# A hybrid mixer kernel on one Trainium2 core: the background modulation taken 1024 columns at a time, in two loads

## The chip, the core and the metric

The kernel runs on one core of a Trainium2 chip. The metric is the device time of one execution in microseconds (us). Five engines work side by side, each through its own queue in a fixed order: TensorE (PE; its weight loads are shown as PEld), VectorE (DVE), ScalarE (ACT), GpSimd (POOL) and SyncE (SP), which issues the DMAs here.

## The reference

Two layers of a diffusion block over 256 context and 1024 latent tokens of width 1024. Before a layer's input is projected, it is normalized and modulated by a vector per stream (one for the latent tokens, one for the context), which comes out of one matrix product per layer:

```python
mod = jax.nn.silu(c) @ w_mod[l] + b_mod[l]            # w_mod[l] is (1024, 3072)
mod_c = jax.nn.silu(c_ctx) @ w_mod[l] + b_mod[l]
sh, sc, gt = jnp.split(mod, 3, axis=-1)               # three parts of 1024 columns
...
hx = _rms(x, norm_w[l]) * (1.0 + sc[:, None, :]) + sh[:, None, :]
ux = _split(hx @ w_in[l], [M_COLS, A_COLS, G_COLS, D_COLS])
outs = [_mlstm_mixer(...), _diff_mixer(...), _gla_mixer(...), _gdn_mixer(...)]
yx = jnp.concatenate([o[1] for o in outs], axis=-1)
x = x + gt[:, None, :] * (yx @ w_out[l])
```

The four mixers are an mLSTM, a differential attention, a gated linear attention (GLA) and a gated DeltaNet. Each takes its own columns of the projection.

## The kernel before

The program is written as strands: functions that each issue their instructions in their own order. A planner (`Issue`) runs while the program is built. It keeps a clock for each engine and for the DMA link, gives every instruction a due time by a rule of costs, and lets the strand go next whose instruction can start first; at equal times the lower rank goes. What comes out is one fixed order for each engine. A change in one strand therefore moves the instructions of all others around it.

In layer 0 two main strands run beside each other. `left` projects the input: products with `w_in` into PSUM tiles `mm`, the lowest-priority work, which fills PE between everything else. When its last product is issued and stored, `left` goes on with the mLSTM: first its states, ten tiles one after another (`m<-k_ident,kq` are a tile's transposes, `m<-pd` its state products), then its outputs (the first is `pp<-kq`). `right` runs a chain: the gates, the DeltaNet with its front (convolutions), decays (`e`), block products (`p<-K`, `po<-K`), an inverse on DVE and POOL (`Y`, `Z`, `ltmp`) and a scan (`p<-S,wq` to `po<-vn,at`); then the attention (`sc<-KT,qt` are its scores), then the GLA (`pd<-qm,km` its first products, `pd<-gv,inner` and `pd<-us,gq` its output products). The output projection is the last: its first half (`o<-w,yT`) beside the mLSTM, the rest after it. Layer 1 goes the same way.

The modulation is a strand of its own. Parts 0 and 1 of layer 0 are needed at once; `modulation` computes them in the first 53 us, 1024 columns wide, one load of 512 KB per step k and four matmuls, which write partitions 0, 32, 64 and 96 of the PSUM tile `ps` (`tile_position=(0, 32 * j)`). The other four parts (part 2 of layer 0, parts 0 to 2 of layer 1) run in the background, at rank 0, from a pool with three buffers `wm` of 128 x 512. Each part is two calls of 512 columns, one after the other; a call takes eight steps, each with one load of 256 KB and two matmuls of 256 columns, and ends with the copies out of `ps` and, for a gate (part 2), with the load of `b_mod`, an addition and the store to `gtd`. A load stands on SP's queue where the strand issues it, after the matmuls of the step before. When all are through, the strand sets "modulated". Two others wait for that: the DeltaNet's inverse before its products on PE, and `QK.rest`, which normalizes and rotates the keys and queries for the attention (two tiles of tokens at a time: load `x`, square, `ss`, the products with `rtk` or `rtq`, transposes `mm<-k_ident,x`, `hi` and `lo`) and uses the room that the modulation's pool gives back.

Of the kernel before, what the change touches and what calls it, by code (L numbers as in the profile page):

```python
# [22 lines left out]
DM = 1024  # L23
# [396 lines left out]
def _build(tc, nc, A, out, root, dbg):  # L420
    q_ = Issue()
    q_.log = dbg.get("log")
    V, S, G, P = (Eng(q_, e, r) for e, r in zip("VSGP", (nc.vector, nc.scalar, nc.gpsimd, nc.tensor)))
# [32 lines left out]
    def mark(label):  # L456
        if q_.me:
            q_.me.label = label

    def dma(dst, src):  # L460
        SP.dma_start(out=dst, in_=src)
# [58 lines left out]
    cvec = cst([128, 8, 2], "cvec")  # L520
# [6 lines left out]
    with ExitStack() as st:  # L527
        ps = Pool(st, "crps", PSUM)([128, 512], "tr")[:, :16]
# [38 lines left out]
    def pc(l, key, i=0, n=1):  # L567
        return pcol[:, l, PR[key] + i:PR[key] + i + n]
# [31 lines left out]
        return A["x"][0, 128 * (t - NCT):128 * (t - NCT) + 128, :]  # L600


    def modulation(l, part, c0, n, p, pps, bufs):

        ps = pps([128, 256], "mod")
        for k in range(8):
            w = p([128, n], "wm", bufs)
            dma(w, A["w_mod"][l, 128 * k:128 * k + 128, 1024 * part + c0:1024 * part + c0 + n])
            if (l, part, k) == (0, 1, 7):
                q_.set("w_mod loads")  # L610
            for j in range(n // 256):
                P.matmul(ps[32 * j:32 * j + 2], cvec[:, k, :], w[:, 256 * j:256 * j + 256],
                         start=(k == 0), stop=(k == 7), tile_position=(0, 32 * j))
        q_.need(("params", l))
        rows = p([128, n], "wm", bufs)[:2].rearrange("p (a b) -> p a b", b=256)
        for j in range(n // 256):
            V.tensor_copy(rows[:, j, :], ps[32 * j:32 * j + 2])
        if part < 2:
            m, k0 = n // 128, c0 // 128
            pt = pps([128, 256], "mod")  # L620
            for j in range(m):
                P.transpose(pt[:, 2 * j:2 * j + 2], rows[:, j // 2, 128 * (j % 2):128 * (j % 2) + 128], ident[:2, :2])
            md = p([128, 8, 2], "md")[:, :m]
            V.tensor_tensor(md, pt[:, :2 * m].rearrange("p (k v) -> p k v", v=2),
                            pc(l, "bm", 8 * part + k0, m).unsqueeze(2).to_broadcast([128, m, 2]), ALU.add)
            for v in range(2):
                if part == 1:
                    V.scalar_tensor_tensor(AB[l][:, 0, v, k0:k0 + m], md[:, :, v], 1.0, pc(l, "nw", k0, m), ALU.add, ALU.mult)
                else:
                    V.tensor_copy(AB[l][:, 1, v, k0:k0 + m], md[:, :, v])  # L630
        else:
            brow = p([128, n], "wm", bufs)[:2]
            dma(brow, A["b_mod"][l:l + 1, 2048 + c0:2048 + c0 + n].to_broadcast([2, n]))
            rv = rows.rearrange("p a b -> p (a b)")
            V.tensor_tensor(rv, rv, brow, ALU.add)
            dma(gtd[l][:, c0:c0 + n], rv)

    def first_norm(hT):
# [6 lines left out]
        def modulations():  # L645
            mark("0mod")
            with ExitStack() as st:
                mp, mps = Pool(st, "wm", side="right"), Pool(st, "mps", PSUM, "right")
                for part in range(2):
                    modulation(0, part, 0, DM, mp, mps, 5)  # L650
            q_.set((0, "AB"))
            q_.need((0, "normed"))

            q_.me.rank = RANK["mod"]
            with ExitStack() as st:
                mp, mps = Pool(st, "wm"), Pool(st, "mps", PSUM)
                q_.set((0, "room"))
                for l, part in ((0, 2), *((l, part) for l in layers if l for part in range(3))):
                    for c0 in (0, 512):
                        modulation(l, part, c0, 512, mp, mps, 3)  # L660
                if "d" in parts:
                    q_.need((0, "front"))
            q_.set("modulated")
        q_.spawn(0, modulations)
        if True:
            st2 = ExitStack()
            xp, pps = Pool(st2, "xn"), Pool(st2, "nps", PSUM)
# [39 lines left out]
        for i in range(len(todo) + 2):  # L707
            if i < len(todo):
                g, k = todo[i]
# [3 lines left out]
            if 0 < i <= len(todo):  # L713
                g, k = todo[i - 1]
                S.copy(hT[0][g][:, k, :], flat[g][:, k, :])
            if i > 1:
                g, k = todo[i - 2]
# [2198 lines left out]
```

## Time and profile before

| | |
|---|---|
| time, median of 3 runs | 2483.91 us (2483.13 to 2484.88) |
| the profiled execution, its own time | 2481.02 us |
| its span, first to last instruction | 2479.1 us |
| PE busy | 2194.1 us, 89% of the span |
| background modulation on PE | from 91.1 us to 339.5 us |
| last gate row of it stored | 342.62 us |
| attention of layer 0, first scores | 686.79 us |
| layer 0's projections end on PE | about 1057 us |
| first mLSTM output product of layer 0 | 1156.01 us |

The trace is one execution. Times of it are from the span's start. A matmul on FP32 operands shows as two records in the trace, where the order of the program has one row; products with the rounded type of `w` and `hT` show as one.

### The profile page before, as it was taken

The numbers are of one execution on the slowest core, as the hardware profiler recorded it, in microseconds if no ns is written. First come the engines' busy times: TensorE is split into PE (matmuls) and PEld (weight loads), VectorE is DVE, ScalarE is ACT, GpSimd is POOL, SyncE is SP. The second block draws the span as 40 slices with busy tenths as digits, with TensorE's granted clock in tenths as the row PEclk, the third lists the DMA queues.
The fourth block names the chain that finished last, engine by engine and source line by source line (L and its number), as shares of the span: only waits on it lengthen the run. The fifth ranks groups of instructions, "written<-read, shape, count | busy, mean of one in ns | idle before, by whom it ended". The sixth has DMA issues, their size and how long they took to land. (4 is left out here: it accounts for less than half of the span.)

```text
span 2479.1 us, 58334 instructions
## 1 busy us (share of the span) xinstructions
PE 2194.1 (89%) x23631; PEld 1772.2 (71%) x23631; DVE 1521.1 (61%) x2786; ACT 980.7 (40%) x2123; POOL 905.9 (37%) x1201
## 2 busy tenths in 40 slices
PE   5899999999988998887877899989899898977989
PEld 2666589888776777775755676888778677765777
DVE  3587449664277773447556486587633587746665
ACT  3346211333266773223334265222332476732240
POOL 2233428363212224422431245373533122255340
PEclk7899999999999999998989999999999999976999
DMA  7446442364423215258963244333343422163595
GB/s 258 123 134 226 155 144 92 104 185 143 131 81 99 71 30 149 72 143 229 267 206 115 68 128 144 127 118 101 119 145 108 126 61 67 48 157 97 153 295 182
DMA packets 343414, 334.61 MB, mean 135 GB/s; under 512 B 88762, under 2 KB 287642, under 8 KB 342634
## 3 DMA queue, kind: packets, MB, share of 16 engines
q1 hardware_dynamic: 343146, 330.88, 44.7%
q8 instruction: 187, 3.06, 0.5%
q14 instruction: 81, 0.66, 0.1%
HBM read 225.98 MB, written 107.43 MB: 134 GB/s over the span
## 5 line engine op out<-in xcount | busy, mean ns | idle before, releaser
L396 PE MATMUL mm<-w,hT 128*128 128x256 f32 x4512 | 635.5, 292 | 16.7 <-ACT st L396 5.8
L396 PEld LDWEIGHTS mm<-w,hT 128*128 128x128 f32 x4512 | 571.1, 193 | 58.3 <-issue 31.4
L396 PE MATMUL mm<-hT,w 128*128 128x512 f32 (+1 forms) x1680 | 389.9, 378 | 13.1 <-ACT hT L396 3.7
L396 PEld LDWEIGHTS mm<-hT,w 128*128 128x128 f32 x1680 | 283.1, 194 | 86.0 <-issue 21.2
L396 DVE TENSOR_REDUCE st<-sc 128x1 f32<-128x1024 f32 (+1 forms) x200 | 200.3, 1026 | 85.8 <-PE sc L396 84.4
L396 ACT ACTIVATE p<-sc,st 128x256 f32<-128x256 f32 (+1 forms) x272 | 211.2, 785 | 74.0 <-DVE st L396 55.4
L396 POOL TENSOR_TENSOR hss<-hss,mhalf 128x2 f32<-128x2 f32 (+2 forms) x72 | 103.3, 1435 | 179.0 <-DVE hss L396 171.1
L396 PE MATMUL o<-wo,yT 128*128 128x512 f32 x540 | 151.3, 420 | 5.1 <-DVE x L396 4.8
L396 PE MATMUL sc<-KT,qt 96*128 96x512 f32 (+1 forms) x400 | 123.7, 399 | 31.0 <-DMA KT<-akh 18.4
L396 POOL TENSOR_TENSOR w<-wr,w 128x512 fp32r<-128x512 f32 x60 | 86.3, 1442 | 158.7 <-ACT w L396 120.7
L396 ACT COPY st<-mm 128x512 f32<-128x512 f32 (+1 forms) x84 | 46.1, 549 | 224.1 <-PE mm L396 182.5
L396 POOL TENSOR_TENSOR ss<-ss,mhalf 128x1 f32<-128x1 f32 (+1 forms) x39 | 67.2, 1723 | 183.8 <-DVE ss L396 172.4
L396 POOL TENSOR_TENSOR st<-st 128x1 f32<-128x1 f32 (+1 forms) x136 | 28.0, 206 | 278.1 <-ACT p L396 202.2
L396 ACT COPY wt<-tr 128x512 f32<-128x512 f32 (+1 forms) x200 | 102.3, 511 | 63.8 <-PE tr L396 63.4
L396 PEld LDWEIGHTS o<-wo,yT 128*128 128x128 f32 x540 | 104.8, 200 | 30.0 <-DVE x L396 4.5
L396 PE MATMUL tr<-k_ident,p 128*128 128x128 f32 x656 | 115.1, 281 | 10.1 <-ACT wt L396 9.8
L396 PE MATMUL o<-w,yT 128*128 128x512 f32 x324 | 103.1, 444 | 20.9 <-DVE st L396 15.1
L396 ACT CAST w<-wr 128x512 fp32r<-128x512 f32 x128 | 76.8, 622 | 92.6 <-DMA wr<-in_w_in 58.4
L396 PEld LDWEIGHTS sc<-KT,qt 96*128 96x128 f32 x400 | 63.5, 195 | 59.3 <-ACT p L396 31.8
L396 PE MATMUL po<-wt,av 128*64 128x128 f32 x1312 | 104.6, 284 | 1.4 <-DVE aacc L396 1.4
L396 DVE SCALAR_TENSOR_TENSOR p<-p,st,p 128x1280 f32<-128x1280 f32 (+1 forms) x72 | 103.0, 1431 | 3.1 <-POOL st L396 3.1
L396 PEld LDWEIGHTS tr<-k_ident,p 128*128 128x128 f32 x656 | 75.8, 141 | 36.6 <-ACT wt L396 21.1
(315 smaller groups left out, 4257.3 us busy)
## 6 DMA issues: line engine op xcount, KB each, us to landing
wr<-in_w_in SPq DMA_DIRECT2D x64, 512.0 KB
wm<-in_w_mod SPq DMA_DIRECT2D x64, 256.0 KB
y<-y SPq DMA_DIRECT2D x36, 256.0 KB
xp<-st SPq DMA_DIRECT2D x18, 512.0 KB
pd<-rs_NG SPq DMA_DIRECT2D x18, 512.0 KB
kq<-kq SPq DMA_DIRECT2D x18, 512.0 KB
x<-xp SPq DMA_DIRECT2D x18, 512.0 KB
wm<-in_w_mod SPq DMA_DIRECT2D x16, 512.0 KB
```

The source lines that it names most:

```text
L396: r = fn(*a, **k)
```

## The change

`modulation` gets its whole width in one call (n = 1024 for all parts) and a second width, `wide`, of one load. In the background `wide` is 512: a step k issues two loads of 256 KB into two `wm` buffers, and then four matmuls, on partitions 0, 32, 64 and 96 of one PSUM tile. There are eight steps per part instead of twice eight. What follows the steps is done in pieces of 512 columns as before, in the new function `mod_piece`, whose body is the old one. In the first 53 us `wide` is 1024, and there the instructions are the same as before. The number of loads (64), of matmuls (128) and of buffers (three) in the background stays.

```diff
-    def modulation(l, part, c0, n, p, pps, bufs):
+    def modulation(l, part, n, p, pps, bufs, wide):
         ps = pps([128, 256], "mod")
         for k in range(8):
-            w = p([128, n], "wm", bufs)
-            dma(w, A["w_mod"][l, 128 * k:128 * k + 128, 1024 * part + c0:1024 * part + c0 + n])
+            ws = []
+            for c in range(0, n, wide):
+                w = p([128, wide], "wm", bufs)
+                dma(w, A["w_mod"][l, 128 * k:128 * k + 128, 1024 * part + c:1024 * part + c + wide])
+                ws += [w[:, i:i + 256] for i in range(0, wide, 256)]
             if (l, part, k) == (0, 1, 7):
                 q_.set("w_mod loads")
             for j in range(n // 256):
-                P.matmul(ps[32 * j:32 * j + 2], cvec[:, k, :], w[:, 256 * j:256 * j + 256],
-                         start=(k == 0), stop=(k == 7), tile_position=(0, 32 * j))
+                P.matmul(ps[32 * j:32 * j + 2], cvec[:, k, :], ws[j], start=(k == 0), stop=(k == 7), tile_position=(0, 32 * j))
         q_.need(("params", l))
-        rows = p([128, n], "wm", bufs)[:2].rearrange("p (a b) -> p a b", b=256)
-        for j in range(n // 256):
-            V.tensor_copy(rows[:, j, :], ps[32 * j:32 * j + 2])
+        pieces = []
+        for c0 in range(0, n, wide):
+            rows = p([128, wide], "wm", bufs)[:2].rearrange("p (a b) -> p a b", b=256)
+            for j in range(wide // 256):
+                V.tensor_copy(rows[:, j, :], ps[32 * (c0 // 256 + j):32 * (c0 // 256 + j) + 2])
+            pieces.append((c0, rows))
+        for c0, rows in pieces:
+            mod_piece(l, part, c0, wide, rows, p, pps, bufs)
+
+    def mod_piece(l, part, c0, n, rows, p, pps, bufs):
         if part < 2:
...
-                    modulation(0, part, 0, DM, mp, mps, 5)
+                    modulation(0, part, DM, mp, mps, 5, DM)
...
-                    for c0 in (0, 512):
-                        modulation(l, part, c0, 512, mp, mps, 3)
+                    modulation(l, part, DM, mp, mps, 3, 512)
```

The planner makes a new order of it. On SP, some 95 us into the program, the loads of the background modulation (`wm<-in_w_mod`) stood one by one between the projection's stores (`dkr`) and the gates' weights (`graw`). Before:

```order
L396 DMA wm_866<-in_w_mod 128x512
L396 DMA dkr_49_126<-st_860 128x512
L396 DMA graw_877<-in_w_in 128x8x32
L396 DMA wm_890<-in_w_mod 128x512
L396 DMA graw_905<-in_w_in 128x8x16
L396 DMA dkr_49_126<-st_900 128x256
L396 DMA wm_916<-in_w_mod 128x512
```

Now:

```order
L396 DMA wm_866<-in_w_mod 128x512
L396 DMA wm_868<-in_w_mod 128x512
L396 DMA dkr_49_126<-st_860 128x512
L396 DMA graw_879<-in_w_in 128x8x32
L396 DMA wm_897<-in_w_mod 128x512
L396 DMA wm_899<-in_w_mod 128x512
L396 DMA graw_908<-in_w_in 128x8x16
```

The loads stand in pairs, and the second of a pair no longer stands behind another load's matmuls. On PE, at the second of these pairs, the matmuls on `wm_897` and `wm_899`, which belong to one step k, stand like this now, with projection matmuls (`mm`) between them:

```order
L396 MATMUL mm_905<-hT_145_226,w_168_288 128x512
L396 MATMUL mod_811<-wm_897,cvec_75 2x256 x2
L396 MATMUL mm_905<-hT_145_226,w_168_288 128x512
L396 MATMUL mm_905<-hT_145_226,w_169_289 128x512
L396 MATMUL mod_811<-wm_899,cvec_75 2x256 x2
L396 MATMUL mm_905<-hT_145_226,w_174_298 128x512 x2
```

They are still two groups of two. Counted through the whole order, the background modulation's 128 matmuls stand in 65 groups before and in 63 now; in two of the 32 steps the four are neighbours. The last of them stands behind 865 projection matmuls before, behind 686 now.

On DVE, where the DeltaNet's inverse begins (`Y<-LT`), the row before it that belongs to `QK.rest` (`ss<-sq`) was the first such unit of keys. Before:

```order
L396 TENSOR_TENSOR Lo_1832<-p_611_3185,Lo_1832 128x2x32
L396 TENSOR_REDUCE ss_3269<-sq_3234 128x16
L396 TENSOR_SCALAR ss_3269<-ss_3269 128x16
L396 TENSOR_TENSOR w_626_3325<-wr_2612,w_625_3324 128x512
L396 STREAM_TRANSPOSE Y_3284<-LT_1831 128x1024 x3
L396 TENSOR_TENSOR x_3227<-x_3227,ss_3269 128x512
L396 TENSOR_TENSOR ltmp_635_3380<-Y_3284,Z_3285 128x31
```

Now:

```order
L396 TENSOR_TENSOR Lo_1973<-p_624_3229,Lo_1973 128x2x32
L396 TENSOR_TENSOR sq_3217<-x_2993,rtk_2699 128x16x8
L396 TENSOR_TENSOR x_2993<-x_2993,rtk_2699 128x512
L396 TENSOR_TENSOR x_2993<-x_2993,sq_3217 128x512
L396 TENSOR_TENSOR lo_3344<-mm_3330,hi_3343 128x512
L396 TENSOR_REDUCE ss_3368<-sq_3366 128x16
L396 TENSOR_SCALAR ss_3368<-ss_3368 128x16
L396 STREAM_TRANSPOSE Y_3317<-LT_1972 128x1024 x3
```

The first three units of keys now stand ahead of the inverse, among the block products, and the fourth has begun.

On PE, where the mLSTM's first transposes (`m_...<-k_ident,kq`) stand, the GLA's output products (`pd<-gv,inner`, `pd<-us,gq`) were going on around them. Before:

```order
L396 MATMUL pd_13065<-us_1995_10692,gq_10673 32x64 x2
L396 MATMUL m_13145<-k_ident_62,kq_13111 128x128 x2
L396 MATMUL pd_13065<-us_1995_10692,gq_10673 32x64 x2
L396 MATMUL pd_13065<-gv_10688,inner_10689 32x64 x4
L396 MATMUL pd_13065<-us_1994_10691,gq_10673 32x64 x4
```

Now:

```order
L396 MATMUL pd_13389<-us_1982_10586,gq_10577 32x64 x4
L396 MATMUL pd_13389<-us_1983_10587,gq_10577 32x64 x4
L396 MATMUL tr_13520<-k_ident_62,y_13473 128x128 x4
L396 MATMUL o_13547<-w_2129_12466,yT_2201_13518 128x512
L396 MATMUL m_13538<-k_ident_62,kq_13528 128x128 x2
L396 MATMUL o_13547<-w_2131_12468,yT_2201_13518 128x512
```

All of the GLA's output products now stand ahead of the mLSTM's first transposes, which are row 7570 of PE's matmuls before and row 7889 now; the rows between are GLA products. At the first mLSTM output product (`pp<-kq`) the two orders meet again, at rows 8109 and 8105. From there to the end of the program they are nearly the same on every engine.

## Rows read from the trace of the kernel before

**Rows 1.** The page, part 1: span, then busy time, share of the span, instructions.

```profile
span 2479.1 us, 58334 instructions
...
PE 2194.1 (89%) x23631; PEld 1772.2 (71%) x23631; DVE 1521.1 (61%) x2786; ACT 980.7 (40%) x2123; POOL 905.9 (37%) x1201
```

**Rows 2.** Busy time of each engine in three stretches.

```profile
core 0: us, PE busy (x) PEld busy (x) DVE busy (x) ACT busy (x) POOL busy (x), PEclk, DMA share, GB/s
...
80.00:345.00 265.00, 254.66 (x1730) 163.39 (x1729) 156.31 (x229) 102.33 (x138) 87.00 (x77) 0.99 0.51 162
...
1057.00:1156.00 99.00, 73.32 (x1243) 57.98 (x1242) 53.46 (x88) 25.95 (x57) 25.50 (x36) 0.86 0.61 164
1156.00:1295.00 139.00, 115.78 (x593) 96.85 (x592) 84.40 (x168) 48.27 (x138) 51.12 (x63) 0.90 0.85 249
```

**Rows 3.** Timeline of PE at the modulation: start, us, instruction, records, [idle before, releaser].

```profile
39.12 0.61 PE L396 MATMUL mod<-wm,cvec 128*2 128x256 f32 x8 [0.27 <-DVE md L396]
...
91.10 0.60 PE L396 MATMUL mod<-wm,cvec 128*2 128x256 f32 x4 [0.28 <-DMA wm<-in_w_mod]
91.63 0.74 PE L396 MATMUL mm<-hT,w 128*128 128x512 f32 x2
...
131.15 1.46 PE L396 MATMUL mod<-wm,cvec 128*2 128x256 f32 x12
132.55 2.13 PE L396 MATMUL mm<-hT,wg 128*128 128x512 f32 x8
```

**Rows 4.** Tile `mod`, 80 to 345 us: its matmuls, min/median/max ns, first and last.

```profile
L396 PE MATMUL mod<-wm,cvec x256: 376/378/631, 91.1 to 339.5; 128*2 128x256 f32 x128
```

**Rows 5.** Waits of PE, 80 to 345 us: total us, times, longest.

```profile
PE mod L396 <- DMA wm<-in_w_mod: 8.0, 12, 1.4
```

**Rows 6.** Timeline of SP at the modulation's end (columns as in rows 3).

```profile
342.62 0.25 SPq L396 DMA_DIRECT2D gt<-wm  x1
...
347.21 0.86 SPq L396 DMA_DIRECT2D x<-in_k_rope  x2
```

**Rows 7.** Timeline of DVE in the DeltaNet's inverse.

```profile
362.07 6.00 DVE L396 STREAM_TRANSPOSE Y<-LT 128x1024 f32<-128x1024 f32 x3
...
374.85 0.59 DVE L396 TENSOR_TENSOR sq<-x,rtk 128x128 f32<-128x128 f32 x1
...
386.22 1.17 DVE L396 TENSOR_TENSOR x<-x,sq 128x512 f32<-128x512 f32 x1
```

**Rows 8.** Timeline of PE from scan to attention, and from attention to GLA.

```profile
661.37 10.29 PE L396 MATMUL mm<-hT,w 128*128 128x512 f32 x43
673.64 5.94 PE L396 MATMUL mm<-w,hT 128*128 128x256 f32 x48 [1.97 <-ACT st L396]
...
686.79 0.77 PE L396 MATMUL sc<-KT,qt 96*128 96x256 f32 x2 [5.69 <-DMA KT<-akh]
...
932.81 15.97 PE L396 MATMUL mm<-w,hT 128*128 128x256 f32 x133
954.50 1.08 PE L396 MATMUL pd<-qm,km 32*32 32x32 f32 x64 [5.71 <-POOL km L396]
```

**Rows 9.** Timeline of PE from the projections' end to the first mLSTM output.

```profile
1057.07 0.31 PE L396 MATMUL pd<-gv,inner 32*32 32x64 f32 x8
...
1059.40 0.68 PE L396 MATMUL pd<-us,gq 32*32 32x64 f32 x16
...
1060.02 0.68 PE L396 MATMUL pd<-us,gq 32*32 32x64 f32 x16
...
1071.06 0.66 PE L396 MATMUL m<-k_ident,kq 128*128 128x128 f32 x2 [4.44 <-DMA kq<-kq]
...
1115.74 0.38 PE L396 MATMUL m<-k_ident,kq 128*128 128x128 f32 x2
...
1129.77 0.70 PE L396 MATMUL m<-pd 128*64 128x65 f32 x8
...
1156.01 1.05 PE L396 MATMUL pp<-kq 128*128 128x128 f32 x8
```

## The prediction

> **What bounds the kernel now.** I read the page first: PE is busy 2194.1 of 2479.1 us, and no other engine passes 61% [rows 1]. A mean over the whole says little, so the table by stretches comes next. While the background modulation runs (80 to 345 us), PE is busy 254.66 of 265.00 us: there the projection is a queue of ready matmuls, and a microsecond less on PE is a microsecond gained. From 1057 to 1156 us, in the mLSTM's states, it is busy 73.32 of 99, so waits decide. In the stretch after that the DMA engines are busy to a share of 0.85 [rows 2]. Third come the timelines of PE at each handover, where I look for rows with idle time in brackets.
>
> The sum is made against the profiled execution: 2481.02 us, that is 2479.1 us of span and 1.9 around it. The median is 2483.91, so I add the change of the sum to the median. A change of 0.2%, about 5 us, is about what a measurement of this kernel can tell from none.
>
> **1. The visits to the narrow matmuls.** What does one cost? A lone pair begins at 91.10, and the projection's next matmul at 91.63: 0.53 us. Four on four partition groups take 0.61 us in the first stage (x8 are records, two to a matmul), as much as a pair's 0.60. Six on the same two groups hold the projection from 131.15 to 132.55: 1.40 us [rows 3]. So what counts is how often PE goes there, and whether the neighbours write other partitions. The tile's 256 records confirm the 128 matmuls [rows 4].
>
> The change says four side by side, but the order does not put them so: strands alternate, and a projection matmul gets between the two pairs of a step. The groups go from 65 to 63. Before: 61 of one or two matmuls at 0.53 (a single one taken like a pair, since the two run side by side), two sixes at 1.40, and two groups of three and four on the same two partition groups, each put at about 1.0, between one pair and three: 32.3 + 2.8 + 2.0 = 37.1 us. After: 60 of one or two at 0.53, two groups of four on four partition groups at 0.53, and one of five whose parts share a partition group, about 1.0: 31.8 + 1.06 + 1.0 = 33.8. Together **-3.3 us**, bounds -1.1 (every group like one pair, 2 x 0.53) and -3.7 (every second pair on a group in use at its own 0.53).
>
> In the Trainium skill, TensorEngine Tiling (Array Packing), section Theoretical Speedup, a small dimension of at most 32 is given up to four times the speed by four tiles. By that, every step of the changed loop would cost one visit, not two; the 0.61 us of the first stage agrees, but the order grants it in two of 32 steps. It is a rival below.
>
> **2. The loads.** They keep their size, number and buffers; what changes is that a pair is issued together. PE waits 8.0 us in 12 waits for `wm` now [rows 5]. With three buffers the second pair finds only one free, and its other load waits for matmuls of the step before. I take 0 change, bounds -4 (half of the waits gone) to +8 (twice as many). The 64 loads pass the same SP queue, with gate weights and stores behind them; projection weights already on chip cover a late one, and without that cover it would be the 8.0 us.
>
> **3. The modulation ends sooner.** Its last matmul stands behind 686 projection matmuls instead of 865. That was at 339.5 us [rows 4]. The 179 matmuls less are 43 us at the 10.29 us for 43 of [rows 8]; with the other work between them I take 50, so the last gate row, which was stored at 342.62, goes out near 290. `QK.rest` waited for that: its first load of `x` stands right behind, at 347.21 [rows 6]. Now it begins as much sooner, and three of its key units go ahead of the DeltaNet's inverse on DVE. A unit has multiplications of 0.59 and 1.17 us among others [rows 7]. I cost this at nothing, since PE has projection matmuls to do meanwhile; without that cover three units would be at least 3 x 1.76 = 5.3 us of a later inverse.
>
> **4. The handovers of the right chain.** With these units done early, the chain of right moves ahead of the filler: the attention's first scores stand behind 2225 projection matmuls instead of 2285, the GLA's first products behind 2841 instead of 2950. Filler that came earlier is missing between stages. From the scan's end to the scores stood 43 matmuls of 512 columns (10.29 us) and some 53 of 256 columns (48 in 5.94, 0.12 us each); now 43 and 24. PE already idled 5.69 us there, so 29 x 0.12 = 3.5 us of cover become idle. From the attention to the GLA the run of 133 at 0.12 us becomes 105, and the idle 5.71 us grows by 28 x 0.12 = 3.4 [rows 8]. Since the total of projection work is the same, idle time here is a loss up to 1057 us: **+6.9 us**, if the chain takes as long as before; 0, if it has become shorter by as much.
>
> **5. GLA ahead of the mLSTM.** The projections end as before, and then `left` begins the states. In the old order 319 products of the GLA stood among the state tiles; now they stand ahead of the first transposes. Their pace is in the rows from 1057.07 on: a period of 24 records, twelve products, takes 0.62 us (1059.40 to 1060.02), 0.051 each. So the transposes, at 1071.06, come 319 x 0.051 = **16.3 us** later. Ahead of them PE idled 4.44 us for a load of `kq` [rows 9]. That load gets more time, but its issue moves as well; I take half, **-2.2**, bounds 0 and -4.4. The states begin -3.3 + 6.9 + 16.3 - 2.2 = 17.7 us later.
>
> **6. The states without GLA.** Before, from 1071.06 to about 1129.8 is 59 us for ten tiles. The first six, with GLA products among them, take 1071.06 to 1115.74, 44.7 us or 7.4 each; the last four 14.1 us or 3.5 each [rows 9]. The moved products are 16.3 us of PE's time, so the least that one expects back is what they cost ahead. More comes back only if the tiles also lost time in waits between the pieces. By the last four rows ten tiles would take 36 us and save 23. The output projection's first half is spread a little more evenly over all tiles in the new order, four to five of its matmuls per tile, so I allow 3.9 us per tile, 39 in all: **-20 us**, bounds 0 and -23.
>
> **Sum.** +17.7 - 20 = **-2.3 us**. At `pp<-kq` the orders meet (1156.01 before [rows 9]) and are nearly the same to the end, so the shift there carries over. 2481.0 becomes 2478.7; on the median 2483.91 - 2.3 = **2481.6 us**.
>
> **The rivals.**
>
> (a) Larger gain: the chain is shorter by what the filler lost, the handovers cost 0, the load of `kq` is there, and the states take 36 us. -3.3 + 16.3 - 4.4 - 23 = -14.4: **2469.5 us**. For it: the 3.5 us per tile are measured, and the units ahead of the inverse are work that need not be done later. Against: the 5.69 and 5.71 us of idle time stand behind chains with little in common with these units.
>
> (b) Slower: the states do not run faster without the GLA, because something other than PE sets their pace, the loads of `kq` first, for one of which PE already waits. The last four tiles were short since their loads had come during the long six. Then ten tiles at 5.5 us (the middle of 3.5 and 7.4) take 55 and save 4: +17.7 - 4 = +13.7, **2497.6 us**. It decides from about 4.1 us per tile on, where 59 - 41 no longer pays for 17.7. For it: PE is busy only 73.32 of 99 us here, and the DMA share is 0.61 [rows 2]. Against: the loads get 17 us more before the first tile.
>
> (c) Four side by side in all steps: if PE ran the two pairs of a step together in spite of what stands between, 63 groups would count as 32. The 31 visits at 0.53 are 16.4 us; of 33 in all, 17.5, some 14 beyond the forecast: **2467.4 us**. The rule of the Trainium skill named above is this case. Against: the row at 91.10 shows a pair paying its 0.53 beside a projection matmul.
>
> (d) It does nothing that lasts: layer 0's shift at `pp<-kq` is eaten or given back in the following stretch, where the DMA engines set the pace at a share of 0.85 [rows 2]: **2484 us**.
>
> **How the numbers follow.** Forecast 0.40, (a) 0.22, (b) 0.20, (d) 0.14, (c) 0.04. The forecast's own terms spread by some 5 us (handovers 0 to 6.9, loads -4 to +8), so of its 0.40 I count 0.14 as faster by over 5 us (below 2478.9), 0.22 as the same and 0.04 as slower. Faster: 0.14 + 0.18 of (a) + 0.04 = 0.36. Same: 0.22 + 0.04 of (a) + 0.14 + 0.02 of (b) = 0.42. Slower (above 2488.9): 0.04 + 0.18 = 0.22. The range takes in most of (a) and the nearer part of (b), 2468 to 2495; outside are the dearer part of (b), about 0.1, and (c) with the far end of (a), about 0.08.
>
> **What the new profile would show.** For step 1: PE's matmuls from 80 us to the modulation's end in 63 groups, a pair still 0.53 us, and waits for `wm` near 8 us. For 3: the last gate row stored near 290 us. For 4: idle time ahead of the scores and of the GLA's first products near 9 us each; 5.7 speaks for (a). For 5: first transposes near 1089 us, no GLA product behind them. For 6: a tile every 3.9 us; 5.5 with waits for `kq` speaks for (b). In the end `pp<-kq` near 1153.7: the end must move by as much as this row, or (d) holds. I would be wrong altogether if the loads in pairs starve the projection of its own weights, so that PE's idle time before 345 us grows, or if the inverse starts later and the filler does not reach that far.

## The result: slower by 1%

The changed kernel takes 2510.53 us in the median of its first four runs (2492.25 to 2518.91) and 2511.88 in six more, against 2483.52 and 2481.26 before. The ratios are 1.0101 (1.0064 to 1.0138) and 1.0121 (1.0087 to 1.0154): 25 to 30 us slower, where 2481.6 was forecast and 2495 was the end of the range. The ten runs differ among themselves by up to 34 us, and the longer ones have the lower mean granted clock of TensorE: of the first four, 2492.25 us at 0.937, 2505.38 at 0.934, 2515.69 and 2518.91 at 0.929.

The profiled execution of the changed kernel is the shortest of the ten, 2492.25 us, so its trace shows less than half of the loss. The page answers to [rows 1], the table by stretches to [rows 2]:

```profile
span 2490.4 us, 58342 instructions
...
PE 2202.7 (88%) x23631; PEld 1779.0 (71%) x23631; DVE 1523.6 (61%) x2781; ACT 988.0 (40%) x2130; POOL 909.2 (37%) x1201
```

```profile
80.00:345.00 265.00, 255.94 (x1806) 163.31 (x1804) 166.06 (x258) 108.17 (x144) 100.96 (x94) 0.99 0.54 172
...
1057.00:1156.00 99.00, 74.35 (x1192) 59.41 (x1190) 54.22 (x83) 27.30 (x55) 31.68 (x41) 0.90 0.55 146
1156.00:1295.00 139.00, 115.83 (x590) 97.66 (x590) 81.97 (x167) 47.34 (x140) 48.43 (x64) 0.87 0.90 255
```

By shares of busy time hardly anything has happened. The change shows in single rows: the modulation's matmuls, PE's waits for their loads (80 to 345 us), and SP's row of the last gate store [rows 4 to 6].

```profile
L396 PE MATMUL mod<-wm,cvec x256: 376/378/587, 88.9 to 283.4; 128*2 128x256 f32 x128
```

```profile
PE mod L396 <- DMA wm<-in_w_mod: 2.0, 3, 1.6
```

```profile
293.25 0.23 SPq L396 DMA_DIRECT2D gt<-wm  x1
...
297.27 0.94 SPq L396 DMA_DIRECT2D x<-in_k_rope  x2
```

The modulation ends 56 us sooner, and the waits for its loads are fewer. Timeline of PE at the two handovers [rows 8], then at the states [rows 9]:

```profile
679.66 0.66 PE L396 MATMUL sc<-KT,qt 96*128 96x256 f32 x2 [3.62 <-issue]
...
950.90 1.08 PE L396 MATMUL pd<-qm,km 32*32 32x32 f32 x64 [5.59 <-POOL km L396]
```

```profile
1097.77 1.12 PE L396 MATMUL tr<-k_ident,y 128*128 128x128 f32 x4 [8.10 <-DMA y<-y]
1099.56 0.79 PE L396 MATMUL o<-w,yT 128*128 128x512 f32 x1 [0.68 <-ACT yT L396]
1101.17 0.69 PE L396 MATMUL m<-k_ident,kq 128*128 128x128 f32 x2 [0.82 <-DMA kq<-kq]
...
1161.13 1.05 PE L396 MATMUL pp<-kq 128*128 128x128 f32 x8
```

The attention starts 7.1 us sooner, the first transposes of the mLSTM come 30.1 us later (1071.06 before), and `pp<-kq`, where the orders meet, is 5.1 us late (1156.01 before). The span is 11.3 us longer.

What the transposes wait for stands on SP's queue. Its timeline between the last store of the projection (`oz<-st`) and the first load of `kq`, before and then now (`y<-hy` is the store of a GLA output, `gz<-gz` the load of the next gate for one, `wdec<-rs_WI` the first of the mLSTM's loads, `y<-y` the load for the output projection's first half):

```profile
1061.62 0.38 SPq L396 DMA_DIRECT2D oz<-st  x1
1062.09 6.34 SPq L396 DMA_DIRECT2D wdec<-rs_WI  x8
1068.47 0.63 SPq L396 DMA_DIRECT2D kq<-kq  x1
```

```profile
1080.50 1.30 SPq L396 DMA_DIRECT2D oz<-st  x1
1085.12 1.81 SPq L396 DMA_DIRECT2D y<-hy  x4
1086.98 3.53 SPq L396 DMA_DIRECT2D gz<-gz  x4
1090.61 4.07 SPq L396 DMA_DIRECT2D wdec<-rs_WI  x6
1094.78 0.59 SPq L396 DMA_DIRECT2D y<-y  x1
...
1097.36 0.63 SPq L396 DMA_DIRECT2D kq<-kq  x1
```

The mLSTM's loads, which came 0.47 us behind the projection's last store, now stand behind DMAs of the GLA's outputs and begin 10.1 us behind it. The first `kq` is issued 28.9 us later than before, and the transposes begin when it lands (the row at 1101.17).

### The profile page after: what moved, and what is told of

Its sections match the earlier page's. It is cut to its first block, busy times and chain, and to the rows that moved or that the text cites. A ratio compares the mean times of both kernels' runs of the same rounds, so it can differ in the third digit from the quotient of the medians.

```text
span 2490.4 us, 58342 instructions
## 1 busy us (share of the span) xinstructions
PE 2202.7 (88%) x23631; PEld 1779.0 (71%) x23631; DVE 1523.6 (61%) x2781; ACT 988.0 (40%) x2130; POOL 909.2 (37%) x1201
## 5 line engine op out<-in xcount | busy, mean ns | idle before, releaser
L396 PE MATMUL mm<-w,hT 128*128 128x256 f32 x4512 | 642.3, 294 | 27.0 <-POOL w L396 10.0
L396 PEld LDWEIGHTS mm<-w,hT 128*128 128x128 f32 x4512 | 575.0, 194 | 70.0 <-issue 30.1
L396 PE MATMUL o<-w,yT 128*128 128x512 f32 x324 | 103.6, 447 | 19.9 <-DVE st L396 12.6
```

The lines of the kernel that those rows point to most:

```text
L396: r = fn(*a, **k)
```

## The experiments

Starts of stages in the profiled executions (us; the first matmul of each kind in the timeline of PE), and what the timed runs gave, as a ratio to the kernel before on the same chip, with its interval. The kernels ran in groups on several chips, so between groups the ratios are to be compared and not the medians. `p<-K` stands for the block products, of which the first, `po<-K`, come some 8 us earlier.

| kernel | `p<-K` | `sc` | `pd<-qm` | `m` | `pp` | span | median | ratio |
|---|---|---|---|---|---|---|---|---|
| before | 313.0 | 686.8 | 954.5 | 1071.1 | 1156.0 | 2479.1 | 2483.9 | |
| before_again | 313.2 | 685.3 | 952.6 | 1064.5 | 1150.8 | 2472.2 | 2476.5 | 0.9991 (0.9968 to 1.0015) |
| after | 313.7 | 679.7 | 950.9 | 1101.2 | 1161.1 | 2490.4 | 2510.5 | 1.0101 (1.0064 to 1.0138) |
| after_again | 316.5 | 705.0 | 977.1 | 1125.6 | 1186.4 | 2524.7 | 2511.9 | 1.0121 (1.0087 to 1.0154) |
| held | 311.5 | 672.4 | 942.9 | 1084.4 | 1162.0 | 2490.2 | 2502.7 | 1.0084 (1.0056 to 1.0113) |
| glued | 363.1 | 744.3 | 1013.7 | 1131.1 | 1213.3 | 2536.0 | 2538.4 | 1.0244 (1.0213 to 1.0274) |
| old_order | 332.4 | 716.9 | 985.5 | 1098.6 | 1182.0 | 2500.8 | 2506.2 | 1.0103 (1.0082 to 1.0124) |
| new_order | 400.4 | 785.2 | 1055.2 | 1209.0 | 1270.6 | 2597.8 | 2591.0 | 1.045 (1.041 to 1.049) |
| covered | 319.5 | 689.7 | 962.4 | 1112.1 | 1174.5 | 2499.5 | 2502.4 | 1.0089 (1.006 to 1.0119) |
| uncovered | 315.1 | 692.5 | 960.2 | 1073.5 | 1157.7 | 2480.2 | 2482.2 | 1.001 (0.9996 to 1.0025) |
| paced | 328.6 | 697.8 | 965.3 | 1080.1 | 1164.5 | 2482.2 | 2483.3 | 1.0014 (0.9995 to 1.0032) |
| spread | 308.7 | 686.1 | 956.8 | 1072.9 | 1157.2 | 2484.0 | 2478.4 | 0.9997 (0.9975 to 1.0019) |
| grouped | 318.5 | 686.2 | 957.0 | 1109.0 | 1174.4 | 2498.0 | 2501.0 | 1.0095 (1.0061 to 1.0129) |
| split | 322.5 | 702.3 | 971.6 | 1084.2 | 1169.5 | 2491.3 | 2487.7 | 1.0029 (1.0009 to 1.0049) |
| h_front | 316.9 | 719.8 | 986.1 | 1098.4 | 1186.5 | 2509.0 | 2490.9 | 1.0042 (1.0024 to 1.0059) |
| h_rest | 325.8 | 694.0 | 965.9 | 1119.2 | 1178.8 | 2507.4 | 2509.5 | 1.0127 (1.0107 to 1.0148) |
| h_gla | 326.4 | 695.5 | 963.4 | 1110.8 | 1172.2 | 2498.1 | 2499.6 | 1.0091 (1.0071 to 1.0112) |

**after_again and before_again: both kernels unaltered.**

> The changed kernel once more, unaltered. Its profiled execution was 11 us over that of before, but the median of its runs 27 us. Theory A (the new order costs time by itself, about 5 us up to the first mLSTM output product and 6 behind it): median 2490 to 2500 when measured in more runs, each near the profiled one, at a mean granted clock near 0.937. Theory B (the runs differ by where the granted clock falls, and the new order loses more of it): runs spread over 2490 to 2520, and the longer a run, the lower its mean granted clock; the added stretches at 0.5 can be read in the trace if this profiled run is one of the long ones.

> The kernel before once more, unaltered, against itself: the ratio should hold 1.000 in its interval, and its width says what a difference must be to count. By both theories the runs lie at 2472 to 2486, with a mean granted clock of 0.938 to 0.944. By theory B they too are longer where the clock is lower.

The profiled run of after_again is the longest (2526.5 us). It goes like the first one until the block products of the DeltaNet (`p<-K`, `po<-Q,K`), at 311 us. Timeline of PE there:

```profile
307.21 3.93 PE L396 MATMUL mm<-w,hT 128*128 128x256 f32 x31
313.38 0.33 PE L396 MATMUL po<-Q,K 64*64 64x64 f32 x4 [2.24 <-DMA Q<-dq]
...
317.26 2.50 PE L396 MATMUL mm<-w,hT 128*128 128x256 f32 x10
```

and its table by stretches (PE's busy time first, then PEld, DVE, ACT and POOL; the granted clock is third from the end):

```profile
310.00:320.00 10.00, 7.76 (x86) 6.08 (x84) 1.67 (x10) 0.59 (x1) 2.60 (x7) 0.77 0.44 148
320.00:330.00 10.00, 10.00 (x102) 7.76 (x94) 3.46 (x17) 0.63 (x1) 2.92 (x1) 0.50 0.26 82
...
360.00:370.00 10.00, 10.00 (x104) 7.47 (x101) 4.88 (x24) 1.70 (x3) 2.89 (x1) 0.50 0.47 159
370.00:380.00 10.00, 8.96 (x88) 7.94 (x87) 4.72 (x16) 1.18 (x3) 3.87 (x4) 0.83 0.15 55
```

PE waits 2.24 us for `Q`, which lands that much later than in the first execution; then the clock is at 1.2 GHz (0.50) from 320 to 370 us although PE is busy all the time. The ten matmuls that take 2.50 us took 1.44 in the first execution. At `p<-S,wq`, behind these products and the inverse, after_again is 518.4 - 495.5 = 22.9 us later than after. Theory B, then, for the spread of the runs. The runs of before_again, too, are longer where the clock is lower (2465.12 us at 0.940, 2488.19 at 0.930). Why the clock falls here is the next question.

**held and glued: the end of the modulation later, and a step's four matmuls together.**

> The changed modulation loop, but its end is made known only when 865 projection matmuls have been issued, as many as stood ahead of it in the kernel before (the last gate row is stored early as in the changed kernel). The GLA's products that stand ahead of the mLSTM's first transposes are then 122 more than before, not 319 more. Theory A, the early end of the modulation as the cause: about 2484 to 2488, and the transposes some 10 us after those of before, between 1075 and 1085 us. Rival, the loop itself (loads in pairs, four side by side) is what costs: as slow as the changed kernel, 2495 to 2510, whatever is held.

```diff
+        if e == "P" and op == "matmul" and outs[0][0].startswith("mm_"):
+            self.mms += 1
+            if self.mms == 865:
+                self.set("hold")
...
                     modulation(l, part, DM, mp, mps, 3, 512)
+                q_.need("hold")
```

> The changed loop with the four matmuls of a step put next to each other on PE, nothing between: 32 groups in the background instead of 63. If a group of four costs one visit (0.53 us), PE saves some 17 us up to the modulation's end; if the two pairs run one after the other, nothing. PE may wait longer for the second load of a step, 5 to 10 us more, as nothing else can go ahead of it. The handovers in the order are those of before (attention behind 2291 projection matmuls, GLA behind 2950, transposes behind 29 more rows). Theory A, the order of GLA and mLSTM costs: 2470 to 2480. Rival, the early release costs in another place, between the block products and the inverse: 2490 or more, since the modulation ends still earlier here.

```diff
-            self.give()
+            if not self.glue:
+                self.give()
...
             for j in range(n // 256):
+                q_.glue = j > 0 and wide < DM
                 P.matmul(ps[32 * j:32 * j + 2], cvec[:, k, :], ws[j], start=(k == 0), stop=(k == 7), tile_position=(0, 32 * j))
+            q_.glue = False
```

Neither lies in the range of its theory A: held is still 20 us slower than before, glued 60. In held the transposes begin at 1084.4, as expected, but the loss stays. No row of the output projection stands ahead of them there, only a wait for `kq`:

```profile
1084.37 0.66 PE L397 MATMUL m<-k_ident,kq 128*128 128x128 f32 x2 [8.85 <-DMA kq<-kq]
```

In glued the modulation outruns its loads. Its waits for `wm`, 80 to 365 us:

```profile
PE mod L398 <- DMA wm<-in_w_mod: 15.4, 13, 2.4
```

and `p<-K` begins 50 us late: from 92.4 us on PE is idle 38.1 us instead of 9.7 and busy 20 us longer, at a mean granted clock of 0.88 instead of 0.99. But where the loads are there, the four do run side by side. Timeline of PE, eight records being four matmuls:

```profile
112.97 0.61 PE L398 MATMUL mod<-wm,cvec 128*2 128x256 f32 x8
113.52 0.49 PE L398 MATMUL mm<-hT,w 128*128 128x512 f32 x1
```

0.55 us from one start to the next, as for a pair. In the Trainium skill, TensorEngine Tiling (Array Packing), section Theoretical Speedup, the gain of four tiles is "Up to 4×"; this row agrees that four matmuls on four column groups cost what one visit costs.

Both edits let the planner make another order again, in layer 1 too, so they change more than they say, and they decide nothing about theory A. All further kernels therefore take the strands in a written sequence: 23593 entries that say which strand goes next, as the planner had chosen it for the one or the other kernel. The edit, with `SCRIPT` the sequence:

```diff
+        idle = [c for c in live if not c[3]]
+        if not idle:
+            want = NAMES[SCRIPT[self.at]]
+            return next(c[2] for c in live if c[2].id == want)
+        live = idle
```

**old_order and new_order: each loop in the other's sequence.** Beyond the edit above, only the sequences are exchanged.

> The changed loop (loads in pairs, four column groups), but the planner is made to take the strands in the very sequence of the kernel before, so that the modulation ends where it ended there; of PE's 16281 rows the last 14816 stand as in the kernel before. Theory C (the order costs, not the loop; in the new order PE waits for Q at the block products and the clock then stays at 0.5 there for some 55 us): as fast as before, 2472 to 2486, no long stretch at 0.5 between 310 and 375 us. Rival (the loop costs by itself, by pairs of loads in three buffers): 2495 or more.

> The loop of before (512 columns per call, two matmuls per load), but the strands are taken in the sequence of the changed kernel; PE's last 15190 rows stand as there. Theory C: as slow as the changed kernel, 2500 to 2515 in the median, spread over more than 20 us, with the stretch at 0.5 from 317 to 372 us in most runs. Rival (the loop costs): 2475 to 2490.

By the words put down ahead, old_order lies in the rival's range (the loop costs), and new_order beyond both. But neither settles it. A strand's turns were made for load, pair, load, pair; in them the new loop has its loads one turn too early or its matmuls too near behind, and the reverse. The stretch from 91.1 us to the first `p<-K` is 241 us in old_order and 309 in new_order, where 222 was usual, and PE's waits for `wm` up to 345 us are 11.7 and 47.6 us. What old_order does show: from `sc` on it takes 2500.8 - 716.9 = 1783.9 us, as before_again (1786.9), not as after (1810.7).

**covered and uncovered: the wait for `Q` taken away, or made.** The edits are moves on PE; the numbers are matmuls in a row, `left` being the projection, `products` the block products.

> The changed kernel with one piece of the order moved: 22 projection matmuls (2.6 us) go ahead of the first block product that needs Q, instead of among the next ones. Theory C: PE waits for Q no more (2.24 us in the long run), the clock stays at 1.0 through the block products, and the median falls by some 20 us to 2488 to 2496. Rival (not the wait but the thin mix of short products and short runs of projection brings the clock down): as the changed kernel, 2505 to 2515.

```diff
 products 4
-left 31, products 12, left 6, products 14, left 10, products 12, left 6
+left 53, products 38
```

> The kernel before with the reverse edit: twelve block products, among them the first six that need Q, are pulled ahead of the 25 projection matmuls (3.2 us) that stood ahead of them, so that PE has to wait about 2 to 4 us for Q at 305 us. Theory C (the wait alone is the trigger): the clock falls to 0.5 there and stays down for tens of us, 2490 to 2510. Rival (in the order of before the longer runs of projection and the modulation's matmuls among the block products hold it up or bring it back at once): 2476 to 2486, a fall of 10 us at most.

```diff
 products 4
-left 25, products 12
+products 12, left 25
```

In covered PE waits for `Q` no more, and yet the clock falls. Its median, 2502.4, lies between the two ranges. Its table by stretches:

```profile
310.00:320.00 10.00, 10.00 (x123) 8.94 (x121) 2.28 (x8) 2.19 (x5) 6.26 (x13) 1.00 0.65 212
320.00:330.00 10.00, 10.00 (x126) 7.42 (x124) 5.42 (x28) 0.63 (x1) 3.29 (x3) 0.57 0.40 133
330.00:340.00 10.00, 10.00 (x87) 7.78 (x88) 4.01 (x15) 0.59 (x1) 0.97 (x2) 0.50 0.15 54
340.00:350.00 10.00, 10.00 (x145) 8.17 (x145) 6.78 (x27) 1.11 (x2) 3.88 (x3) 0.91 0.47 159
```

In uncovered PE waits, 1.17 us, and the clock dips and is back at once:

```profile
300.00:310.00 10.00, 8.84 (x82) 6.18 (x81) 3.09 (x6) 2.07 (x4) 1.79 (x2) 0.87 0.66 214
310.00:320.00 10.00, 10.00 (x125) 7.80 (x123) 3.39 (x20) 1.73 (x3) 2.51 (x2) 0.96 0.50 161
320.00:330.00 10.00, 10.00 (x154) 7.41 (x152) 3.34 (x20) 0.59 (x1) 0.00 (x0) 1.00 0.43 137
```

So, as far as one execution of each shows, the wait alone is not what keeps the clock down; theory C falls in that form. The Trainium skill, TensorE: Matmul & The Clock Gate, section HAM oscillation — how this bites in real kernels, lays such falls to waits for DMA between short pieces of work; in after_again the fall begins behind such a wait (2.24 us), covered shows a fall without one, and there the measurement decides.

**paced and spread: the modulation alone moved.** In paced the modulation's instructions stand where they stand in the changed kernel, counted in projection matmuls, and all others are in the old sequence. In spread its loads are on the old places, and the four matmuls of a step on that of every second old pair.

> The changed loop at the pace that it has in the changed kernel (its last matmul behind 686 projection matmuls), but all other strands in the very sequence of the kernel before, so that only the modulation's own instructions stand elsewhere; the block products at 313 to 356 us then have no matmuls of the modulation among them, as in the changed kernel. Theory D (what held the clock up there in the kernel before were the modulation's matmuls among the short products): the clock falls to 0.5 for 15 to 60 us there in at least part of the runs, 2485 to 2505, and from the attention on the times of before. Theory E (the runs of 16 projection matmuls between the products hold it; the new order has runs of 6 to 10): no long stretch at 0.5, 2474 to 2484. If the loop itself cost time, the stretch from 91 to 313 us would be longer than 222 us.

> The changed loop spread over the time that the old one took: each load at the place of an old load, the four matmuls of a step next to each other at the place of every second old pair; all other strands in the sequence of the kernel before. 28 visits of PE to the background modulation instead of 65. If a visit of four costs what one of two costs (0.53 us), PE needs 222 - 18 = 204 us from 91 us to the first block product, and the whole takes 2460 to 2468, if the block products keep the clock with half as many visits among them; by theory D with visits too few to hold it, 15 to 20 us more. If the pairs of a step do not run together, 2476 to 2484.

paced settles the loop as far as the times can: with the modulation as fast as in the changed kernel and nothing else moved, the time is that of before, 1.0014 with 1 in the interval, whose upper end is 8 us. (The stretch from the first background matmul to `p<-K` is 13 us longer, 235.1 us for 221.9, which was put down as the sign that the loop costs. 5.4 us of it are busy time, since more of the modulation stands ahead of the products, and 7.8 are idle time. The way from there to the scan is 8 us shorter, 181.5 for 189.7.) Among its block products there is no matmul of the modulation, and the clock stays at 1.00 from 300 to 400 us: theory D falls, again by one execution. spread settles the four side by side:

```profile
121.05 0.61 PE L573 MATMUL mod<-wm,cvec 128*2 128x256 f32 x8
121.60 0.62 PE L573 MATMUL mm<-hT,w 128*128 128x256 f32 x3
```

From 91.1 us to the first `p<-K` PE is busy 199.8 us instead of 212.2 (added up from its timeline), 12.4 less, but idle 17.8 instead of 9.7. The stretch is 4 us shorter, and the whole as long as before within its interval, not the 2460 to 2468 us that were expected.

**grouped and split: the length of the projection's runs among the block products.** grouped is the changed kernel's sequence with five moves, split that of paced with seven:

> The changed kernel with five moves among the block products: the projection's runs of 6 to 10 matmuls between groups of 12 to 16 block products are put together to runs of 16 to 37 between groups of 26 to 28, as the kernel before has them; everything behind the products stands as in the changed kernel. Theory E (short runs between the products let the clock fall and keep it low): no stretch at 0.5 over 10 us between 313 and 375 us, the spread of the runs falls to that of before, and the median by 15 to 20 us to 2488 to 2496. What is left above before is then the order from the attention on. Rival (the early load and work of the keys and queries, or chance): as the changed kernel, 2505 to 2515.

```diff
-left 31, products 12, left 6, products 14, left 10, products 12, left 6, products 16, left 10, ...
+left 37, products 26, left 16, products 28, left 16, products 26, left 21, products 28, ...
```

> The reverse, on the kernel that ran as fast as before (the changed loop at its own pace, all else in the sequence of before): seven runs of 12 to 17 projection matmuls among the block products are cut into runs of 4 to 10, with 12 to 16 products between, as the changed kernel has them. Theory E: the clock falls to 0.5 for 15 to 60 us between 320 and 375 us in most runs, median 2495 to 2508. Rival (the length of the runs doesn't matter): 2478 to 2488 as without the cuts.

```diff
-left 16, products 24, left 16, products 24, left 16, products 24, ...
+left 10, products 12, left 6, products 12, left 10, products 12, left 6, products 12, ...
```

In split PE doesn't wait, and the clock falls. Its table by stretches, where paced had 1.00 throughout:

```profile
320.00:330.00 10.00, 10.00 (x126) 7.84 (x126) 3.33 (x20) 1.14 (x2) 2.51 (x2) 0.78 0.40 140
330.00:340.00 10.00, 10.00 (x95) 7.60 (x95) 3.14 (x20) 0.59 (x1) 0.00 (x0) 0.50 0.15 54
340.00:350.00 10.00, 10.00 (x81) 8.40 (x81) 1.86 (x12) 0.00 (x0) 0.00 (x0) 0.53 0.14 52
350.00:360.00 10.00, 10.00 (x143) 8.28 (x141) 2.23 (x14) 0.59 (x1) 0.00 (x0) 1.00 0.15 54
```

In grouped PE waits for `Q`, and the clock dips and comes back:

```profile
310.00:320.00 10.00, 7.84 (x89) 6.48 (x88) 1.67 (x10) 0.00 (x0) 4.29 (x10) 0.83 0.51 162
320.00:330.00 10.00, 10.00 (x141) 8.14 (x140) 4.13 (x23) 1.22 (x2) 3.32 (x3) 0.83 0.41 133
330.00:340.00 10.00, 10.00 (x151) 8.13 (x151) 8.16 (x34) 1.70 (x3) 1.81 (x3) 1.00 0.49 159
```

So the length of the runs has an effect on the clock in these executions, as theory E says. In the times it is small: by the ratios split lies 4 us above paced and grouped 6 below after_again, with intervals that overlap. Both times miss theory E: split lies where its rival put it, and grouped was expected at 2488 to 2496. Most of the 25 to 30 us is elsewhere.

**h_front, h_rest and h_gla: the two sequences joined.** A sequence is followed up to a matmul of `right`, and from there the other one, without what has been issued.

> The strands are taken in the sequence of the changed kernel (with the block products in long runs, as in grouped) up to the attention's first scores, and from there in the sequence of the kernel before. Theory F (the rest of the 30 us is the order behind the attention's start: filler missing in it, GLA products ahead of the mLSTM's transposes, the wait for y): as fast as before or a little faster, 2472 to 2486. Rival G (the front: keys and queries ahead of the inverse, and what the loads of the modulation take from others): 2493 to 2503, as grouped.

> The reverse: all strands but the modulation in the sequence of the kernel before up to the attention's first scores, and from there in the sequence of the changed kernel. Theory F: 2495 to 2505. Rival G: 2476 to 2488. By the forecast on record (states without GLA give back what the later start costs), too, 2478 to 2488.

> As h_rest, but the sequence of the kernel before holds through the attention, up to the first product of the GLA, and that of the changed kernel comes behind it: only GLA, mLSTM states and the output's first half are in the new order. If the GLA ahead of the mLSTM costs (terms 5 and 6 of the forecast, which should cancel): 2493 to 2503. If the attention's stage does (its filler and waits): 2476 to 2488.

h_rest is as slow as the changed kernel: with the old order up to the attention's first scores and the new one behind them, the whole loss is there, as theory F says (2495 to 2505 was expected, 2509.5 measured). Its other half holds less well: h_front is not as fast as before, but 10 us slower (1.0024 to 1.0059). Against paced, h_rest loses 1.0127 - 1.0014, about 28 us; h_gla, with only GLA and states in the new order, 19; h_front 7. The profiled run of h_front is its longest, 2511 us, and has the clock at 0.50 through most of the block products, with a wait for `Q` and the long runs of grouped; so long runs make the fall rarer at most. The parts of h_rest and h_front add up to 35 us, more than the 25 to 30 of the whole: they overlap, or the front gives back some of its cost later.

The table of starts says the same in all kernels. From `sc` to the end of the span, the eight executions in the old sequence (before, before_again, old_order, uncovered, paced, spread, split, h_front) take 1783.9 to 1797.9 us, the six in the new one (after, after_again, new_order, covered, grouped, h_rest) 1809.7 to 1819.7: 24 us more in the mean. Of these, 3 lie in the attention (`sc` to `pd<-qm`), 14 from there to `pp`, and 7 behind it. That h_rest loses 9 us more than h_gla by the ratios, with intervals that overlap, doesn't make the attention dear: in their traces it takes 271.9 and 267.9 us.

What happens between the GLA's first product and `pp<-kq` is in two tables by stretches, each cut at the first transposes of the mLSTM, and in two rows of h_gla's timeline. First paced, then h_gla:

```profile
965.30:1080.10 114.80, 98.41 (x3263) 89.30 (x3263) 61.94 (x110) 38.85 (x75) 55.12 (x71) 0.95 0.33 94
1080.10:1164.50 84.40, 66.72 (x925) 51.06 (x926) 45.35 (x76) 21.62 (x50) 23.18 (x35) 0.83 0.63 181
```

```profile
963.40:1110.80 147.40, 121.53 (x3895) 110.21 (x3895) 77.48 (x118) 37.81 (x70) 73.70 (x88) 0.86 0.33 89
1110.80:1172.20 61.40, 45.08 (x288) 32.81 (x289) 40.72 (x67) 20.69 (x49) 16.66 (x30) 0.83 0.71 200
```

```profile
1107.43 1.12 PE L568 MATMUL tr<-k_ident,y 128*128 128x128 f32 x4 [7.74 <-DMA y<-y]
...
1110.84 0.69 PE L568 MATMUL m<-k_ident,kq 128*128 128x128 f32 x2 [0.82 <-DMA kq<-kq]
```

The states give back 84.4 - 61.4 = 23 us, but the way to them is 147.4 - 114.8 = 32.6 us longer: 23.1 of busy time (121.53 - 98.41; the moved products, and a clock of 0.86 instead of 0.95) and 9.5 of idle time. Of the latter 7.74 us is one wait for `y`, the load for the first half of the output projection, whose first rows stand ahead of the transposes now. But this wait doesn't hold the transposes back. They begin when `kq` lands, in h_gla as in the changed kernel and in every other profiled execution, 2.6 to 4.7 us behind its issue. What PE does for `y` passes in time in which it would wait for `kq` anyway (on SP the load of `y` and one of `st` put 1.3 us ahead of it), and in held, where `y` comes later, PE does wait for `kq`, 8.85 us. The load of `kq` is late on SP. In the eight executions in the old sequence the mLSTM's loads begin 0.47 us behind the projection's last store; in the new one, h_gla too, 7.9 to 10.1 us behind it, behind the GLA's `y<-hy` and `gz<-gz`. No kernel moved these rows of SP alone, so what that would give back is not shown.

## Why the prediction was wrong

The time lies outside the range, and on the other side of the forecast. The step that failed is the load in step 5: the forecast let the transposes gain 2.2 us on the load of `kq`, and they lost 7.1. By the steps, in the changed kernel's profiled execution where no other is named:

- **1, the visits.** The price was right: a pair or a four costs 0.53 to 0.55 us, and the new order has hardly any fours. Whether the 3.3 us arrived, no run shows by itself; paced puts the loop as a whole between a gain of 1 and a loss of 8 us.
- **2, the loads.** PE's waits went from 8.0 us to 2.0, beyond the bound of -4, a gain.
- **3, the modulation's end.** The place was right (last gate row at 293.25, forecast 290), and in this execution the scan starts sooner than before (495.5 for 502.7). What the forecast had no term for is the clock: in after_again, the same program, the scan starts 22.9 us later, behind block products at 0.50, which is 1.2 GHz. h_front puts the new front at some 7 us.
- **4, the handovers.** Wrong: 3.62 and 5.59 us of idle time, not 9 each; the chain became shorter by what the filler lost, as rival (a) has it. But the attention, from its first scores to the GLA's first product, took 271.2 us instead of 267.7, with 30.2 us of idle time instead of 22.6, and the forecast had no term for it.
- **5, GLA ahead of the mLSTM: the step that failed.** What stands ahead of the transposes came out near the forecast, in part by luck, since its terms had the loss in other places: the last GLA product ends on PE at 1089.67 instead of 1066.62, 23.0 us later, where -3.3 + 6.9 + 16.3 = 19.9 was forecast. (Of the 319 moved rows 314 are GLA products; the other five are the `tr<-k_ident,y` and the `o<-w,yT` that the order of the change shows there.) But from that end to the transposes it is 11.5 us, where it was 4.44 and 2.2 was forecast. The forecast named both sides ("That load gets more time, but its issue moves as well") and took a gain. The load is issued 28.9 us later than before, behind the GLA's DMAs on SP, whose order there the forecast does not show. The wait on PE's row did shrink (4.44 to 0.82 us), but because PE waited for `y` in the meantime. The states begin 30.1 us late, not 17.7; 9.3 of the 12.4 us between are the load.
- **6, the states.** Right in kind: 25 us back, beyond the bound of 23, where 20 was forecast; 23 in h_gla.
- **The carry-over.** `pp<-kq` was 5.1 us late instead of 2.3 early, and the end 11.3. Behind `pp<-kq` PE is busy 9.2 us longer and idle 3 us less, at a granted clock of 0.92 instead of 0.93.

Rival (b) had the sign and half of the loss, but not the mechanism: the load of `kq` sets when the states start, and the states themselves did run faster. Rival (c) wanted the two pairs of a step to run together in spite of what stands between; glued and spread show four that are neighbours at the price of a pair, which this order hardly has.

What stays open: which part of the fall at the block products is due to the wait for `Q` and which to the short runs (each is seen without the other, and with a wait the clock came back at once in uncovered and grouped and not in after_again and h_front), why the attention takes 3 us more, and why the new order loses 7 us in the mean behind `pp<-kq`, where it is nearly the old one. Of h_gla against paced these are 8.2 us (2498.1 - 1172.2 against 2482.2 - 1164.5), of which 7.4 is busy time of PE, at a granted clock of 0.92 for 0.93. No kernel tried beat the one before; spread equals it.

## What to carry to other kernels

Where a planner makes the order, a change of a loop is a change of order first: time the loop in the old order (paced), and the new order piece by piece (h_front, h_rest, h_gla), before the loop is praised or blamed. Work that moves ahead of a chain takes its DMAs with it: read on the DMA queue, too, what now stands ahead of the load that the chain starts with. The last wait on PE can mislead there: PE waited 8.10 us for `y` and 0.82 for `kq`, and it was `kq` that decided. And look at the granted clock beside the busy time: PE was busy 10.00 of 10.00 us at 0.50, and the ten matmuls that took 1.44 us at full clock took 2.50.

## What the runs showed of the hardware

The granted clock stayed at 0.50 for some 50 us while PE was busy without a gap, in after_again, and for some 20 us in covered and split, where the table shows no idle time just before the fall. What PE did then were block products of 64 x 32 and 64 x 64, 12 to 16 in a row, between runs of 6 to 10 projection matmuls; with runs of 16 it was mostly, not always (h_front), at 1.00. That these products and not something else beside them keep the clock down is not shown. The executions of the changed program lay 34 us apart (2492 to 2526 us), those of before_again 23 us (2465 to 2488).

Four matmuls of two rows each on four column groups took 0.61 us, as two did, also when they come from two loads; that was known from the first stage [rows 3], and it held in the background where the four were neighbours (glued, spread).
